# A hybrid decoder block on one core: another form of the norm behind the output projection, and two planner rules

## The chip, the core and the metric

One core of a Trainium2 chip runs the kernel. The metric is the device time of one execution in microseconds. The kernel's engines are called as in the profile: PE (TensorE, matmuls; PEld is its weight load), DVE (VectorE), ACT (ScalarE), POOL (GpSimd) and SP (SyncE, which here only issues DMAs).

## The reference

One layer of a decoder block on x of 512 tokens by 1,024 features, in float32. A vector c gives six modulation vectors; a mixer (a convolution branch and latent attention, gated and merged, then one output projection) and an MLP of width 4,096 follow, each between norms:

```python
mod = silu(c) @ w_ada + b_ada        # shift1, scale1, gate1, shift2, scale2, gate2
h = rms_norm(x, g_pre_mix) * (1.0 + scale1) + shift1
y = token_mixer(h, ...)              # ends in (g_a * y_a + g_b * y_b) @ w_out
x = x + gate1 * rms_norm(y, g_post_mix)

h = rms_norm(x, g_pre_mlp) * (1.0 + scale2) + shift2
y = square(relu(h @ w_mlp_in)) @ w_mlp_out
x = x + gate2 * rms_norm(y, g_post_mlp)
```

`rms_norm(x, g)` is `x * rsqrt(mean(x * x) + eps) * g` over the features.

## The kernel before

**Number format.** Float32 products are made of three matmuls (`mm3`): each operand is split into a high part in fp32r and a low part, and high x high, high x low and low x high are summed in PSUM. The split costs ACT a cast and DVE a subtraction per operand, so nearly all weights and activations pass through ACT and DVE on their way to PE.

**Recording and planning.** No engine is called directly. `act`, `dve`, `pe`, `pool` and `sp` record operations into a `Planner`; `record` (from L262) works out on which earlier operations each one depends, by the regions that it reads and writes, and gives it a cost by a table (`cost`). `plan` (from L340) then simulates the engines: PE takes ready operations by their rank in the program, the others by their due time, worked back from PE's. `issue` sends everything in the order that came out; whatever the operation, its line in the profile is that of the sending call, L421. So a change of a dependency, a cost or a landing time changes the order of instructions on every engine, though not the instructions. Loads are modelled by `o.dma` and a landing time `o.t1`; at most DEPTH of them are in flight on SP.

**Memory.** `fa` hands out pieces of one float32 arena (`f_arena` in the profile), `ra` of an fp32r arena (`r_arena`), `pb` the eight PSUM banks of 512 float32 columns. `stats` and `mod` hold small vectors.

**The stage behind the output projection.** Tokens lie in four row tiles t of 128 (NT = 4), features in KD = 8 blocks k of 128. The product with w_out is made in halves nh of 512 columns: first the halves 0 of all tiles, 96 matmuls of 512 columns; then `late_mod` turns the last modulation vectors (parts 2, 3 and 4 of w_ada) into G1, which is gate1 times the norm's gain, broadcast to 128 rows, and into columns of `mod`; then halves 1, 24 matmuls of 512 columns a tile, 96 in all. When a tile's second half is done, its norm runs, row by row: sum of squares, a power -0.5 on POOL, product with G1, addition to the residual xr, a second norm for the MLP, whose result is transposed on PE (eight 128x128 transposes a tile, four to a PSUM bank, tiles in pairs tp) and evacuated with scale and shift into h2, feature-major, in high and low parts. ACT writes v and the high part, DVE the low part; each covers 256 columns, the pair's tokens.

**The MLP.** The first four blocks of the hidden layer are computed in two steps of 256 tokens, so that they need only the first pair's h2 at first: these are the 256-column matmuls on `r_arena` (360 of them). All later ones have 512 or 256 columns by a Strassen-like scheme. While it runs, `ada_units((5,))` computes the last part of the modulation, gate2, on DVE, from 1 MB loads of two row blocks of w_ada each.

These lines are the norm of tile t before, which the change rewrites (`rstd` is the Identity on ACT with scale and epsilon, and the power on POOL):

```python
                for nh in range(2):
                    act.activation(fa.v(j), pb.v(ys[t, nh]), AF.Square, accum_out=s[:, nh:nh + 1])
```

Of the kernel before, what the change touches and what calls it, by code (L numbers as in the profile page):

```python
# [14 lines left out]
AF = mybir.ActivationFunctionType  # L15
ALU = mybir.AluOpType

P = 128
T = 512
NT = T // P  # L20
D = 1024
KD = D // P
# [33 lines left out]
ADAS = (1, 1, 0, 4)  # L56
KGRP = ((1,), (2,), (3,), (4,), (5,), (6,), (7,))
HL, SQ = 5e3, False
ADD, LATE5 = 2.6, 1
HX, HA, HG, HC = 1.2e5, 1e5, 3e3, 1.1e5  # L60

# [108 lines left out]


class Op:
    __slots__ = ("i", "eng", "fn", "a", "k", "cost", "post", "deps", "succ", "dead", "t0", "t1", "ndep", "ready", "dma", "rank", "hurry", "bufs", "raw")


class Planner:
# [6 lines left out]
    def __init__(self, nc, spaces):  # L183
        self.spaces = spaces
        self.real = dict(pe=nc.tensor, act=nc.scalar, dve=nc.vector, pool=nc.gpsimd, sp=nc.sync)
        self.ops = []
        self.last_w = {}
        self.reads = {}
        self.boost = 0
        self.hurry = 0.0  # L190
        self.after = None
        self.slack = 0.0

    class Engine:
        def __init__(self, plan, name):
# [76 lines left out]
    def record(self, eng, fn, a, k):  # L272
# [3 lines left out]
        outs, ins = [], []  # L276
# [9 lines left out]
        o = Op()  # L286
        o.i, o.eng, o.fn, o.a, o.k = len(self.ops), eng, fn, a, k
        o.succ, o.dma, o.rank, o.hurry = [], None, len(self.ops) - self.boost, self.hurry
        o.cost, o.post = self.cost(eng, fn, outs, ins, k)
        o.post += self.slack if eng == "pool" else 0.0  # L290
        if fn == "dma_start":
            b = 4
# [29 lines left out]
        for nm, units in wr:  # L322
            lw, rs = self.last_w[nm], self.reads[nm]
            for u in units:
                lw[u] = o.i
                rs.pop(u, None)
        deps.discard(o.i)
        if self.after is not None:
            deps.add(self.after)
# [5 lines left out]
    def plan(self):  # L335
# [29 lines left out]
        while len(order) < len(ops):  # L365
# [3 lines left out]
            for e in self.NAMES:  # L369
                if free[e] <= now and heaps[e]:  # L370
                    o = ops[heapq.heappop(heaps[e])[1]]
                    o.t0 = now
                    free[e] = now + o.cost
                    if o.dma:
                        st = max(now + 1100.0, dma_free)
                        dma_free = st + o.dma
                        o.t1 = dma_free + 1100.0
                        landed.append(o.t1)
                        free[e] = max(free[e], landed[-DEPTH])
                    else:  # L380
                        o.t1 = free[e] + o.post
                    order.append(o)
                    for s in o.succ:
                        q = ops[s]
                        q.ndep -= 1
                        q.ready = max(q.ready, o.t1 if (q.eng != o.eng or o.dma) else free[e] if e == "pe" else max(free[e], o.t1 - 30))
                        if not q.ndep:
                            heapq.heappush(future, (q.ready, q.i))
# [37 lines left out]
def tile_hybrid_block(  # L426
# [48 lines left out]
    def emit(past, replay):  # L475
# [713 lines left out]
        def ada_units(parts):  # L1189

            for part in parts:
                acc = ada_acc[part] = fa.alloc(D)
                for u in range(4):
                    b = fa.alloc(2 * D)
                    v = fa.v(b, "p (j n) -> p j n", j=2)
                    sp.dma_start(out=v, in_=w_ada[u * 256:(u + 1) * 256, part * D:(part + 1) * D].rearrange("(j p) n -> p j n", p=P))
                    for jj in range(2):
                        j = u * 2 + jj
                        if j == 0:
# [201 lines left out]
        xr = []  # L1401
# [31 lines left out]
        for tp in range(2):  # L1433
            xn = []
            for t in (2 * tp, 2 * tp + 1):
# [2 lines left out]
                    if t == NT - 1 and k % 2 == 1:  # L1438
                        wo[k // 2].free()
                s = stat(6)  # L1440
                j = fa.alloc(512)
                for nh in range(2):
                    act.activation(fa.v(j), pb.v(ys[t, nh]), AF.Square, accum_out=s[:, nh:nh + 1])
                fa.free(j)
                act.activation(s[:, 2:3], s[:, 0:1], AF.Identity, scale=0.25 / D, bias=epsc[:, 0:1])
                rstd(s[:, 3:4], s[:, 1:2], 0.25 / D, s[:, 2:3])
                y = fa.alloc(D)
                for nh in range(2):
                    sl = slice(nh * 512, (nh + 1) * 512)
                    dve.scalar_tensor_tensor(fa.v(y)[:, sl], pb.v(ys[t, nh]), s[:, 3:4], fa.v(G1)[:, sl], op0=ALU.mult, op1=ALU.mult)  # L1450
                    pb.free(ys[t, nh])
                dve.tensor_tensor(fa.v(xr[t]), fa.v(xr[t]), fa.v(y), ALU.add)
                act.activation(fa.v(y), fa.v(xr[t]), AF.Square, accum_out=s[:, 4:5])
                rstd(s[:, 5:6], s[:, 4:5], 1.0 / D)
                dve.tensor_scalar(fa.v(y), fa.v(xr[t]), s[:, 5:6], None, ALU.mult)
                for nh in range(2):
                    sl = slice(nh * 512, (nh + 1) * 512)
# [12 lines left out]
            for k2 in range(KD // 2):  # L1470
# [5 lines left out]
                for q in range(2):  # L1476
                    k = 2 * k2 + q
                    ps, v = pb.v(b)[:, q * 256:(q + 1) * 256], k4(fa.v(h2f[k // 4]))[:, k % 4, hsl]
                    hb, lb = (ra.v(z)[:, hsl] for z in h2[k])
                    if k == 0:  # L1480
                        act.activation(hb, ps, AF.Identity, scale=mod[:, 3, k:k + 1], bias=mod[:, 2, k:k + 1])
                        dve.tensor_scalar(v, ps, mod[:, 3, k:k + 1], mod[:, 2, k:k + 1], ALU.mult, ALU.add)
                    else:
# [12 lines left out]
        G2, fin = None, []  # L1496

        late = ada_units((5,))

        def blocks_of(wsrc, k0):  # L1500

# [183 lines left out]
        for ch in range(NCH):  # L1685
# [3 lines left out]
            for n0 in range(0, HPC, GRP):  # L1689
# [12 lines left out]
                ws = ws0 if ch == 0 and n0 == 0 else hid_weights(ch * HPC + n0, GRP)  # L1702
                step = 256 if ch == 0 and n0 == 0 else T
                for t0 in range(0, T, step):
                    for i in range(GRP):
                        for k in range(KD):
                            mm3(pb.v(bs[i])[:, t0:t0 + step], ws[i - i % 2, k // 4](k % 4, (i % 2) * P, P), h2s(k, t0, step),
                                k == 0, k == KD - 1)
                for w in ws.values():
# [131 lines left out]
```

## Time and profile before

| | us |
|---|---|
| median of 3 runs | 811.71 (811.28 to 812.33) |
| the profiled execution | 812.9 |
| its span in the profile | 810.8 |
| PE busy | 791.7 (98%) |
| DVE busy | 732.8 (90%) |
| ACT busy | 476.7 (59%) |
| POOL busy | 62.6 (8%) |

The mean granted PE clock was 0.996 of full speed. Some 2.1 us of the execution lie outside the span. In the profile's chain of work that ended last PE has 84% and DVE 9%. In timelines and groups, a row has the operation, output and inputs by name, and the number of instructions; a bracket holds the idle time ahead of it and what ended that. As all operations have line L421 (L433 in the changed kernel, which is twelve lines longer up to there), operations are told apart by engine, names and shapes.

### The profile page before, as it was taken

The numbers are of one execution on the slowest core, as the hardware profiler recorded it, in microseconds if no ns is written. First come the engines' busy times: TensorE is split into PE (matmuls) and PEld (weight loads), VectorE is DVE, ScalarE is ACT, GpSimd is POOL, SyncE is SP. The second block draws the span as 40 slices with busy tenths as digits, with TensorE's granted clock in tenths as the row PEclk, the third lists the DMA queues.
The fourth block names the chain that finished last, engine by engine and source line by source line (L and its number), as shares of the span: only waits on it lengthen the run. The fifth ranks groups of instructions, "written<-read, shape, count | busy, mean of one in ns | idle before, by whom it ended". The sixth has DMA issues, their size and how long they took to land.

```text
span 810.8 us, 11964 instructions
## 1 busy us (share of the span) xinstructions
PE 791.7 (98%) x4450; PEld 689.5 (85%) x4450; DVE 732.8 (90%) x1040; ACT 476.7 (59%) x790; POOL 62.6 (8%) x121
## 2 busy tenths in 40 slices
PE   5999999999999999999999999999999999999996
PEld 2788988889897888888888879988998899889985
DVE  2799999999999999999896578899999968996998
ACT  5555463365885247238243276677667766777842
POOL 2001010000000000000000020001002200320023
PEclk9999999999999999999999999999999999999999
DMA  8999433112252261343798062139826950895095
GB/s 256 314 272 356 142 121 107 53 53 78 92 170 78 79 181 53 104 157 122 291 395 280 1 208 97 60 83 305 314 78 141 272 168 17 179 281 177 1 190 135
DMA packets 100108, 130.99 MB, mean 162 GB/s; under 512 B 8561, under 2 KB 67282, under 8 KB 100050
## 3 DMA queue, kind: packets, MB, share of 16 engines
q1 hardware_dynamic: 93714, 118.69, 44.3%
q0 software_dynamic: 6336, 11.54, 8.8%
q8 instruction: 35, 0.57, 0.3%
q14 instruction: 23, 0.19, 0.1%
HBM read 109.23 MB, written 20.97 MB: 161 GB/s over the span
## 4 chain that ended last, share of the span: by engine, by line
PE 84%; DVE 9%; ACT 2%; issue 2%; DMA 2%; SPq 0%; DVEq 0%; POOLq 0%; POOL 0%
PE psum L421 84%; DVE f_arena L421 5%; DVE r_arena L421 4%; ACT f_arena L421 1%; ACT r_arena L421 1%; DMA rows<-in_g_pre_mix_dram 1%; DMA f_arena<-in_w_in_dram 1%; SPq L421 0%; DVEq L1836 0%; POOLq L1836 0%; DVE mod L421 0%; POOL stats L421 0%; ACT stats L421 0%; DVE stats L421 0%; DVE cols L421 0%
## 5 line engine op out<-in xcount | busy, mean ns | idle before, releaser
L421 PE MATMUL psum<-r_arena 128*128 128x512 f32 (+3 forms) x4108 | 752.3, 344 | 1.8 <-ACT f_arena L421 0.7
L421 PEld LDWEIGHTS psum<-r_arena 128*128 128x128 f32 x4108 | 649.8, 190 | 87.7 <-ACT r_arena L421 1.7
L421 ACT CAST r_arena<-f_arena 128x1024 fp32r<-128x1024 f32 (+4 forms) x249 | 236.2, 967 | 152.8 <-PE psum L421 92.8
L421 DVE TENSOR_TENSOR r_arena<-f_arena,r_arena 128x1024 fp32r<-128x1024 f32 (+5 forms) x259 | 276.1, 1097 | 27.2 <-PE psum L421 15.6
L421 DVE SCALAR_TENSOR_TENSOR f_arena<-f_arena,cw 128x512 f32<-128x512 f32 x240 | 164.9, 745 | 0.0
L421 DVE TENSOR_TENSOR f_arena<-f_arena 128x1024 f32<-128x1024 f32 (+3 forms) x108 | 114.3, 1076 | 3.8 <-ACT f_arena L421 2.4
L421 ACT ACTIVATE f_arena<-f_arena 128x512 f32<-128x512 f32 (+4 forms) x121 | 71.4, 609 | 41.6 <-DVE f_arena L421 40.8
L421 ACT COPY f_arena<-psum 128x512 f32<-128x512 f32 (+4 forms) x107 | 57.5, 550 | 48.3 <-PE psum L421 43.6
L421 DVE SCALAR_TENSOR_TENSOR f_arena<-f_arena,cT 128x256 f32<-128x256 f32 (+1 forms) x70 | 54.3, 800 | 1.5 <-DMA f_arena<-in_w_ada_dram 1.2
L421 POOL DMA_DIRECT2D y_spill<-f_arena x40 | 34.7, 868 | 263.6 <-ACT f_arena L421 263.6
L421 ACT ACTIVATE f_arena<-psum 128x512 f32<-128x512 f32 x43 | 25.3, 594 | 38.8 <-PE psum L421 38.7
L421 PE MATMUL psum<-ident,f_arena 128*128 128x128 f32 (+1 forms) x234 | 33.4, 279 | 5.2 <-DVE f_arena L421 5.2
L421 PEld LDWEIGHTS psum<-ident,f_arena 128*128 128x128 f32 (+1 forms) x234 | 27.4, 143 | 10.9 <-DVE f_arena L421 5.7
L421 DVE TENSOR_TENSOR r_arena<-psum,r_arena 128x512 fp32r<-128x512 f32 (+2 forms) x57 | 35.9, 656 | 0.3
L421 DVE TENSOR_TENSOR f_arena<-psum,f_arena 128x512 f32<-128x512 f32 (+1 forms) x35 | 23.2, 673 | 13.7 <-PE psum L421 13.7
L421 ACT CAST r_arena<-psum 128x512 fp32r<-128x512 f32 (+2 forms) x57 | 29.9, 563 | 8.9 <-PE psum L421 8.6
L421 POOL TENSOR_TENSOR stats<-stats,nhalf 128x1 f32<-128x1 f32 (+1 forms) x17 | 15.9, 942 | 169.6 <-ACT stats L421 159.4
L421 POOL TENSOR_TENSOR lns<-lns,nhalf 128x4 f32<-128x4 f32 x1 | 2.0, 2002 | 249.3 <-DVE lns L421 249.3
L421 ACT ACTIVATE r_arena<-f_arena 128x256 fp32r<-128x256 f32 (+3 forms) x17 | 10.9, 643 | 14.0 <-DVE f_arena L421 11.3
L421 DVE CUSTOM_DVE_ANT_0 f_arena<-psum,mask 128x128 f32<-128x128 f32 (+3 forms) x32 | 14.9, 484 | 0.1
L421 DVE TENSOR_SCALAR f_arena<-f_arena,stats 128x1024 f32<-128x1024 f32 x8 | 6.0, 751 | 8.5 <-POOL stats L421 8.5
L421 DVE SCALAR_TENSOR_TENSOR f_arena<-f_arena 128x512 f32<-128x512 f32 (+1 forms) x18 | 13.1, 748 | 0.2 <-ACT f_arena L421 0.2
(96 smaller groups left out, 204.0 us busy)
## 6 DMA issues: line engine op xcount, KB each, us to landing
f_arena<-in_w_ada_dram SPq DMA_DIRECT2D x16, 1024.0 KB, 6.5
f_arena<-in_w_mlp_in_dram SPq DMA_DIRECT2D x32, 512.0 KB, 6.0
f_arena<-in_w_mlp_out_dram SPq DMA_DIRECT2D x32, 512.0 KB, 5.9
f_arena<-in_w_in_dram SPq DMA_DIRECT2D x24, 512.0 KB, 4.8
y_spill<-f_arena POOLq DMA_DIRECT2D x40, 256.0 KB, 6.4
f_arena<-in_w_ada_dram SPq DMA_DIRECT2D x24, 256.0 KB, 5.9
f_arena<-in_x_dram SPq DMA_DIRECT2D x8, 512.0 KB, 7.1
h_spill<-r_arena SPq DMA_DIRECT2D x16, 256.0 KB, 7.0
```

What stands on the lines that cost most here:

```text
L421: getattr(self.real[o.eng], o.fn)(*o.a, **o.k)
```

## The change

**The norm.** Before, DVE multiplied the PSUM halves by the norm's factor and by G1 in one instruction each, once the power was there, added the result to xr (1,024 wide), ACT squared the sum (1,024 wide), POOL took the second power. Now DVE multiplies both halves by G1 at once (`tensor_tensor`, which needs no statistic) into y; ACT squares PSUM with the scale folded in; after the power two instructions on DVE make y times factor plus xr, half by half; ACT squares half 0 and adds epsilon, and DVE's `tensor_tensor_reduce` squares and sums half 1, starting from ACT's value; POOL takes the power. The scaling by it is as before. The scratch j lies in the fp32r arena.

**The planner.** With EXCL, operations of different engines on one PSUM bank depend on each other in the plan, whatever columns they touch: each waits for the run of operations that another engine had last on the bank. With LAG, the loads by SP into the float32 arena that are recorded after `late = ada_units((5,))`, that is the MLP's, land 3,000 ns later in the plan. **Loads.** With AJ = 1 each 1 MB load of w_ada in `ada_units` becomes two of 512 KB. KOUT and VK have the values that leave the code as it was.

```diff
+EXCL = True
+LAG, AJ = 3000.0, 1
+KOUT, VK = False, (0,)
...
+        o.lag = self.lag if fn == "dma_start" and eng == "sp" and outs[0].tensor.name.startswith("f_arena") else 0.0
...
+        if EXCL:
+            for bank in {u // 2 for nm, units in rd + wr if nm.startswith("psum") for u in units}:
+                runs = self.runs.setdefault(bank, [(None, []), (None, [])])
+                if runs[1][0] != eng:
+                    runs[:] = [runs[1], (eng, [])]
+                deps.update(runs[0][1])
+                runs[1][1].append(o.i)
...
-                        o.t1 = dma_free + 1100.0
+                        o.t1 = dma_free + 1100.0 + o.lag
...
-                    sp.dma_start(out=v, in_=w_ada[u * 256:(u + 1) * 256, part * D:(part + 1) * D].rearrange("(j p) n -> p j n", p=P))
+                    src = w_ada[u * 256:(u + 1) * 256, part * D:(part + 1) * D].rearrange("(j p) n -> p j n", p=P)
+                    for jj in range(0, 2, AJ):
+                        sp.dma_start(out=v[:, jj:jj + AJ], in_=src[:, jj:jj + AJ])
...
-                j = fa.alloc(512)
-                for nh in range(2):
-                    act.activation(fa.v(j), pb.v(ys[t, nh]), AF.Square, accum_out=s[:, nh:nh + 1])
-                fa.free(j)
-                act.activation(s[:, 2:3], s[:, 0:1], AF.Identity, scale=0.25 / D, bias=epsc[:, 0:1])
-                rstd(s[:, 3:4], s[:, 1:2], 0.25 / D, s[:, 2:3])
                 y = fa.alloc(D)
+                j = ra.alloc(512)
                 for nh in range(2):
                     sl = slice(nh * 512, (nh + 1) * 512)
-                    dve.scalar_tensor_tensor(fa.v(y)[:, sl], pb.v(ys[t, nh]), s[:, 3:4], fa.v(G1)[:, sl], op0=ALU.mult, op1=ALU.mult)
+                    act.activation(ra.v(j), pb.v(ys[t, nh]), AF.Square, scale=0.5 * D ** -0.5, accum_out=s[:, nh:nh + 1])
+                    if nh == 0:
+                        act.activation(s[:, 0:1], s[:, 0:1], AF.Identity, bias=epsc[:, 0:1])
+                    dve.tensor_tensor(fa.v(y)[:, sl], pb.v(ys[t, nh]), fa.v(G1)[:, sl], ALU.mult)
                     pb.free(ys[t, nh])
-                dve.tensor_tensor(fa.v(xr[t]), fa.v(xr[t]), fa.v(y), ALU.add)
-                act.activation(fa.v(y), fa.v(xr[t]), AF.Square, accum_out=s[:, 4:5])
-                rstd(s[:, 5:6], s[:, 4:5], 1.0 / D)
+                rstd(s[:, 2:3], s[:, 1:2], 1.0, s[:, 0:1])
+                for nh in range(2):
+                    sl = slice(nh * 512, (nh + 1) * 512)
+                    xs_ = fa.v(xr[t])[:, sl]
+                    dve.scalar_tensor_tensor(xs_, fa.v(y)[:, sl], s[:, 2:3], xs_, op0=ALU.mult, op1=ALU.add)
+                    if nh == 0:
+                        act.activation(ra.v(j), xs_, AF.Square, scale=D ** -0.5, accum_out=s[:, 3:4])
+                        act.activation(s[:, 3:4], s[:, 3:4], AF.Identity, bias=epsc[:, 0:1])
+                    else:
+                        dve.tensor_tensor_reduce(ra.v(j), xs_, xs_, 1.0 / D, s[:, 3:4], ALU.mult, ALU.add, s[:, 4:5])
+                        pool.tensor_tensor(s[:, 5:6], s[:, 4:5], nhalf[:, :1], ALU.pow)
+                ra.free(j)
                 dve.tensor_scalar(fa.v(y), fa.v(xr[t]), s[:, 5:6], None, ALU.mult)
```

What the plan makes of it is seen in the orders. PE behind the output projection, before: the rows of 512 columns are the second halves of the four tiles, 96 in all; the groups of transposes (`ident`) between them are first those of `late_mod` (16), then those of the normalized tiles; the rows of 256 columns are the first MLP matmuls.

```order
166 L421 MATMUL psum<-ident,f_arena 128x128 x16
167 L421 MATMUL psum<-r_arena 128x512 x62
168 L421 MATMUL psum<-ident,f_arena 128x128 x4
169 L421 MATMUL psum<-r_arena 128x512 x2
170 L421 MATMUL psum<-ident,f_arena 128x128 x2
171 L421 MATMUL psum<-r_arena 128x512
172 L421 MATMUL psum<-ident,f_arena 128x128 x2
173 L421 MATMUL psum<-r_arena 128x512 x21
174 L421 MATMUL psum<-ident,f_arena 128x128 x8
175 L421 MATMUL psum<-r_arena 128x512 x10
176 L421 MATMUL psum<-r_arena 128x256 x30
177 L421 MATMUL psum<-ident,f_arena 128x128 x8
```

PE at the same place in the changed kernel:

```order
160 L433 MATMUL psum<-ident,f_arena 128x128 x16
161 L433 MATMUL psum<-r_arena 128x512 x53
162 L433 MATMUL psum<-ident,f_arena 128x128 x8
163 L433 MATMUL psum<-r_arena 128x512 x20
164 L433 MATMUL psum<-ident,f_arena 128x128 x8
165 L433 MATMUL psum<-r_arena 128x512 x23
166 L433 MATMUL psum<-r_arena 128x256 x16
167 L433 MATMUL psum<-ident,f_arena 128x128 x8
168 L433 MATMUL psum<-r_arena 128x256 x50
169 L433 MATMUL psum<-ident,f_arena 128x128 x8
```

Tile 0's transposes stood behind 62 of the 96 matmuls, in three pieces, tile 1's behind 85; now behind 53 and 73, each in one piece. Tiles 2 and 3 follow behind 16 and 66 short matmuls; it was 30 and 68 before.

DVE at the norms of tiles 0 and 1, before (`stats` holds the row statistics):

```order
444 L421 SCALAR_TENSOR_TENSOR f_arena<-psum,stats,f_arena 128x512 x2
445 L421 TENSOR_TENSOR f_arena<-f_arena 128x1024
446 L421 TENSOR_SCALAR f_arena<-f_arena,stats 128x1024
447 L421 SCALAR_TENSOR_TENSOR f_arena<-psum,stats,f_arena 128x512 x2
448 L421 TENSOR_TENSOR f_arena<-f_arena 128x1024
449 L421 TENSOR_TENSOR r_arena<-f_arena,r_arena 128x1024
450 L421 TENSOR_SCALAR f_arena<-f_arena,stats 128x1024
```

DVE there in the changed kernel (ISA with `stats` is the reduction, and the row behind it the read of its sum):

```order
470 L433 TENSOR_TENSOR f_arena<-psum,f_arena 128x512
471 L433 SCALAR_TENSOR_TENSOR f_arena<-f_arena,stats 128x512 x2
472 L433 ISA r_arena,stats<-f_arena,stats 128x512
473 L433 ISA stats 128x1
474 L433 TENSOR_SCALAR f_arena<-f_arena,stats 128x1024
475 L433 TENSOR_TENSOR f_arena<-psum,f_arena 128x512
476 L433 SCALAR_TENSOR_TENSOR f_arena<-f_arena,stats 128x512 x2
477 L433 ISA r_arena,stats<-f_arena,stats 128x512
478 L433 ISA stats 128x1
479 L433 TENSOR_SCALAR f_arena<-f_arena,stats 128x1024
```

The addition of 1,024 columns is gone; a product from PSUM and a reduction have come. Only one product a tile stands here: those of the halves 0 have moved up among `late_mod`'s operations.

PE in its first part, before (`cT` is c in columns; these matmuls make the first modulation vectors):

```order
6 L421 MATMUL psum<-ident,f_arena 128x128 x6
7 L421 MATMUL psum<-ones,f_arena 128x1 x2
8 L421 MATMUL psum<-f_arena,cT 1x256 x8
9 L421 MATMUL psum<-ident,f_arena 128x128 x6
10 L421 MATMUL psum<-ones,f_arena 128x1 x2
```

And now:

```order
6 L433 MATMUL psum<-ident,f_arena 128x128 x6
7 L433 MATMUL psum<-ones,f_arena 128x1 x2
8 L433 MATMUL psum<-ident,f_arena 128x128 x5
9 L433 MATMUL psum<-f_arena,cT 1x256 x8
10 L433 MATMUL psum<-ident,f_arena 128x128 x12
```

Five transposes have moved ahead of the matmuls with `cT`.

More of the change, by code (lines that the diff above doesn't have):

```diff
@@ L172 @@
 class Op:
-    __slots__ = ("i", "eng", "fn", "a", "k", "cost", "post", "deps", "succ", "dead", "t0", "t1", "ndep", "ready", "dma", "rank", "hurry", "bufs", "raw")
+    __slots__ = ("i", "eng", "fn", "a", "k", "cost", "post", "deps", "succ", "dead", "t0", "t1", "ndep", "ready", "dma", "lag", "rank", "hurry", "bufs", "raw")
 class Planner:
@@ L191, in __init__ @@
         self.after = None
-        self.slack = 0.0
+        self.runs = {}
+        self.lag = self.slack = 0.0
     class Engine:
@@ L1479, in emit @@
                     hb, lb = (ra.v(z)[:, hsl] for z in h2[k])
-                    if k == 0:
+                    if k in VK:
                         act.activation(hb, ps, AF.Identity, scale=mod[:, 3, k:k + 1], bias=mod[:, 2, k:k + 1])
@@ L1498, in emit @@
         late = ada_units((5,))
+        plan.lag = LAG
         def blocks_of(wsrc, k0):
@@ L1704, in emit @@
                 for t0 in range(0, T, step):
-                    for i in range(GRP):
-                        for k in range(KD):
+                    for i, k in ([(i, k) for k in range(KD) for i in range(GRP)] if step < T and KOUT
+                                 else [(i, k) for i in range(GRP) for k in range(KD)]):
+                        if True:
                             mm3(pb.v(bs[i])[:, t0:t0 + step], ws[i - i % 2, k // 4](k % 4, (i % 2) * P, P), h2s(k, t0, step),
```

## The prediction

> **What bounds the kernel now.** I read the page first, for the busy shares, then PE's waits, then PE's row in stretches, and last the chain inside one stretch. The page:
>
> ```profile
> span 810.8 us, 11964 instructions
> PE 791.7 (98%) x4450; PEld 689.5 (85%) x4450; DVE 732.8 (90%) x1040; ACT 476.7 (59%) x790; POOL 62.6 (8%) x121
> ```
>
> PE is busy for 791.7 of 810.8 us. So the change can only gain what PE loses: in waits, in a slower clock, in a tail. PE's waits in the whole span (total us, times, longest), the larger ones:
>
> ```profile
> PE psum L421 <- DVE f_arena L421: 5.2, 1, 5.2
> PE psum L421 <- DMA c<-in_c_dram: 2.3, 1, 2.3
> PE psum L421 <- ACT f_arena L421: 1.1, 2, 0.7
> PE psum L421 <- DMA rows<-in_g_pre_mix_dram: 1.0, 1, 1.0
> PE psum L421 <- DVE r_arena L421: 0.6, 1, 0.6
> PE psum L421 <- DVE mod L421: 0.4, 1, 0.4
> PE psum L421 <- ACT r_arena L421: 0.4, 1, 0.4
> ```
>
> The 5.2, the 2.3, the 1.0 and the 0.4 for mod stand in the first 25 us, while inputs land. Of the rest, 0.7 for ACT f_arena and 0.6 for DVE r_arena stand at one place, behind the norm. The stretches around it (PE busy, PEld, DVE, ACT, POOL, granted clock, DMA share, GB/s):
>
> ```profile
> 420.00:440.00 20.00, 20.00 (x90) 16.58 (x89) 19.81 (x23) 9.89 (x12) 0.00 (x0) 1.00 1.06 368
> 460.00:475.70 15.70, 15.70 (x74) 12.98 (x74) 9.53 (x13) 6.88 (x17) 3.70 (x5) 1.00 0.27 100
> 475.70:479.50 3.80, 3.78 (x20) 2.63 (x18) 3.80 (x6) 3.80 (x8) 0.42 (x1) 1.00 0.68 235
> 479.50:483.00 3.50, 2.03 (x12) 1.41 (x11) 3.13 (x6) 3.44 (x11) 1.40 (x1) 1.00 0.69 235
> 483.00:486.40 3.40, 3.40 (x16) 3.40 (x17) 3.34 (x5) 3.40 (x8) 0.53 (x2) 0.51 0.85 272
> 486.40:493.00 6.60, 6.60 (x58) 6.60 (x57) 5.37 (x8) 2.09 (x5) 1.88 (x1) 0.99 0.57 192
> 580.00:600.00 20.00, 20.00 (x169) 20.00 (x168) 18.18 (x18) 14.06 (x20) 0.00 (x0) 1.00 0.45 160
> ```
>
> A 512-column matmul takes 20/90 = 0.222 us, a 256-column one 20/169 = 0.118. In 479.5 to 483 PE did 12 short matmuls, worth 1.42 of 3.50 us: 2.08 lost. In 483 to 486.4 it did 16, worth 1.89 of 3.40, at clock 0.51: 1.51 lost. Together **3.59 us**, the loss of this stage. The waits are the cause; the slow clock follows them. PE there:
>
> ```profile
> 476.14 1.09 PE L421 MATMUL psum<-ident,f_arena 128*128 128x128 f32 x8
> 480.54 1.71 PE L421 MATMUL psum<-r_arena 128*128 128x256 f32 x9 [0.60 <-DVE r_arena L421]
> 482.97 4.15 PE L421 MATMUL psum<-r_arena 128*128 128x256 f32 x20 [0.72 <-ACT f_arena L421]
> ```
>
> The transposes of row tile 1 start at 476.14; behind them stand, by the order of before, ten long matmuls (2.2 us), and then MLP matmuls that need h2, evacuated from these transposes by ACT and DVE. So h2 is late, because the normalized tile 1 was.
>
> **The norm, tile by tile.** The chain before, in DVE's rows and ACT's (the last two are ACT's evacuation of h2, quoted for later):
>
> ```profile
> 462.84 1.41 DVE L421 SCALAR_TENSOR_TENSOR f_arena<-psum,stats,f_arena 128x512 f32<-128x512 f32 x2 [0.92 <-POOL stats L421]
> 464.28 1.23 DVE L421 TENSOR_TENSOR f_arena<-f_arena 128x1024 f32<-128x1024 f32 x1
> 468.14 0.75 DVE L421 TENSOR_SCALAR f_arena<-f_arena,stats 128x1024 f32<-128x1024 f32 x1 [2.63 <-POOL stats L421]
> 475.33 0.75 DVE L421 TENSOR_SCALAR f_arena<-f_arena,stats 128x1024 f32<-128x1024 f32 x1 [0.44 <-POOL stats L421]
> ...
> 461.16 0.60 ACT L421 ACTIVATE f_arena<-psum 128x512 f32<-128x512 f32 x1 [6.95 <-PE psum L421]
> 461.66 0.19 ACT L421 ACTIVATION_READ_ACCUMULATOR f_arena<-psum 128x1 f32 x1
> 461.88 0.29 ACT L421 ACTIVATE stats<-stats 128x1 f32<-128x1 f32 x1
> 465.54 1.06 ACT L421 ACTIVATE f_arena<-f_arena 128x1024 f32<-128x1024 f32 x1 [3.37 <-DVE f_arena L421]
> 466.60 0.60 ACT L421 ACTIVATE f_arena<-psum 128x512 f32<-128x512 f32 x1
> 481.92 1.00 ACT L421 ACTIVATE f_arena<-psum,mod 128x256 f32<-128x256 f32 x2
> 482.82 0.71 ACT L421 CAST r_arena<-f_arena 128x256 fp32r<-128x256 f32 x2
> ```
>
> From the last Square on PSUM to the normalized tile: tile 0 461.16 to 468.89, 7.7 us; tile 1 466.60 to 476.08, 9.5 us. Nothing runs beside it: Square, power, two products, a 1.23 us addition, a 1.06 us Square, power, scaling.
>
> Prices of the new instructions, from the nearest forms in the run (count, total us, mean ns, idle before):
>
> ```profile
> L421 DVE TENSOR_TENSOR f_arena<-psum,f_arena 128x512 f32<-128x512 f32 x33 | 22.3, 689 | 13.7 <-PE psum L421 13.7
> L421 DVE SCALAR_TENSOR_TENSOR f_arena<-f_arena,stats 128x512 f32<-128x512 f32 x8 | 5.7, 755 | 0.1
> L421 DVE CUSTOM_DVE_ANT_0 r_arena<-f_arena,stats 128x512 fp32r<-128x512 f32 x3 | 2.2, 758 | 0.0
> L421 DVE DVE_READ_ACCUMULATOR2_ANT stats<- 128x1 f32 x4 | 0.4, 92 | 0.0
> L421 DVE SCALAR_TENSOR_TENSOR f_arena<-psum,stats,f_arena 128x512 f32<-128x512 f32 x8 | 5.6, 746 | 1.4 <-POOL stats L421 1.4
> L421 DVE TENSOR_SCALAR f_arena<-psum,mod 128x256 f32<-128x256 f32 x2 | 1.1, 545 | 1.7 <-ACT f_arena L421 1.7
> ```
>
> Counted from the Square's start: the first power is there at 1.7, as before (462.84 - 461.16; the Identity now comes earlier, which I leave out). The product with G1 is 0.69 long and is meanwhile done, at 0.7 beside the Square or at 0.60 + 0.69 = 1.3 behind it. The second is likelier: the last row above is DVE reading one half of a bank and waiting for ACT, whose read of the other half ended then. Both are under 1.7, so it costs nothing. Two multiply-adds end at 1.7 + 2 x 0.755 = 3.2. ACT squares half 0 from 2.45: a 512-wide Square, its read and Identity are 0.60 + 0.19 + 0.29, to 3.5. DVE's reduction of half 1 waits 0.3 for that seed and ends, with its read, at 3.5 + 0.76 + 0.09 = 4.4. From a statistic's end to DVE through POOL took 462.84 - 462.17 = 0.67; the scaling starts at 5.05 and ends at **5.8**. So tile 0 is 1.9 us earlier and tile 1, were nothing in its way, 3.7; tile 1's last matmul comes 24 x 0.222 = 5.3 us after tile 0's, while DVE holds tile 0 until 5.8, so 0.5 go, and I take 0.3 more for queueing: about **2.9**. Seen against the 1.32 us of waits listed (or 2.08 lost), this suffices, if PE's order uses it.
>
> It does: the transposes of tiles 0 and 1 now stand behind 53 and 73 of the 96 long matmuls (62 and 85 before). Tile 0's last matmul is the 24th, so 29 x 0.222 = 6.4 us pass against a chain of 5.8; tile 1's is the 48th, 25 x 0.222 + 1.1 for tile 0's eight transposes = 6.6 against 5.8. And 23 long matmuls, not 10, now cover the evacuation: 13 x 0.222 = 2.9 us more. Evacuating two k blocks took ACT 1.00 + 0.71 us, so eight blocks need some 6.9 us from the transposes; 23 x 0.222 + 21 x 0.118 = 7.6 us pass until the last block is first read. Tight, since tile 2's Square (0.6 + 0.19) also stands in ACT's way. I leave **0.5 us** of waits, between 0 and the old 1.3. The slow stretch I take as gone with them.
>
> How sure are the 1.51 us? They come from one execution, at 812.9 us, which is 1.2 above the median of the timed ones. The Trainium skill ("TensorE: Matmul & The Clock Gate", Part 1) states that the gate judges a free-running window of about 3.4 us, so that the same kernel is slowed for differing stretches from run to run. By that sentence the stretch could be missing in the median run, and the sum would be 1.5 smaller. The trace agrees with it in part only: the stretch at 0.51 is 3.4 us long, but it followed waits of 1.3 us, not an idle window. I count the 1.51 in full; the other case is the first rival.
>
> DVE's work: per tile 2 x 0.689 + 2 x 0.755 + 0.758 + 0.092 for 2 x 0.746 + 1.22, +1.0 us, 4.1 in all. Of it the products of the first halves, 4 x 0.689 = 2.8, stand earlier, where DVE idles. In 460 to 493 DVE was busy for 9.53 + 3.80 + 3.13 + 3.34 + 5.37 = 25.2 of 33 us; now 26.5 of 29.3 (33 less the gain). It fits, with less room than before: the cover that could fail.
>
> **The other edits.** Six groups of transposes become four in this stage. A change of kind costs about 0.09 us: a long matmul between two groups took 0.31, not 0.222:
>
> ```profile
> 470.62 0.48 PE L421 MATMUL psum<-r_arena 128*128 128x512 f32 x1
> 470.93 0.38 PE L421 MATMUL psum<-ident,f_arena 128*128 128x128 f32 x2
> ...
> 465.54 0.83 SPq L421 DMA_DIRECT2D out_dram<-f_arena  x2
> ...
> DVE r_arena L421 <- PE psum L421: 6.8, 6, 1.7
> ```
>
> That is **-0.2**. At the start five transposes now stand ahead of the matmuls that waited 0.4 for mod: 5 x 0.14 (1.09/8) = 0.7 us covers it, **-0.4**, between 0 and -0.4. Halved w_ada loads are 16 more issues on SP at 0.83/2 = 0.42 us, 6.7 us spread over hundreds: nothing; without cover one late load, 0.4. The bank rule and the landing margin issue no instruction; they alter order alone. PE's remaining small waits (0.4 for ACT r_arena, 0.4 more for ACT f_arena) may go or grow: 0, between -1 and +1. In the MLP PE doesn't wait (20.00 of 20.00 us in the row of 580 to 600), so a margin can gain nothing there. Could it lose? DVE's orders differ by at most five places, and DVE itself waits for PE to free buffers (last row above, of 640 to 720: 6.8 us), so it works ahead: 0, at worst +1.2, one 1024-wide operation. The tail holds the same operations: 0.
>
> Sum: -3.6 + 0.5 - 0.2 - 0.4 = **-3.7 us**. The profiled run took 812.9, 2.1 more than its span; it should come to 809.2, the span to 807.1. The median was 811.7, so **808.0**. A measurement here can tell about 0.2%, 1.6 us.
>
> **The rivals.** *The clock's share isn't gained (0.17).* Whether a stall halves the clock may hang on where it falls, so that the timed runs of before mostly lack the slow stretch; or what is left of the waits still trips it. The 1.51 us drop out of the sum: 3.7 - 1.5 = 2.2, 809.5. For it: the profiled execution is slower than the timed ones by nearly that much. Against: the stall that comes before it stands in the order of every run alike. *The stall moves (0.11).* Tiles 2 and 3 are now transposed behind 16 and 66 short matmuls, where 30 and 68 stood; 14 x 0.118 = 1.7 us less for tile 2's chain. If tile 2 comes late by all of that and the clock follows (1.5), 3.2 of 3.6 is given back: 811.3. *More goes (0.12).* All of PE's small waits vanish, the two of 0.4 too, and nothing is left in the stage: 808.0 - 0.5 - 0.8 = 806.7. For it: the whole order is planned anew. Against: the same could open others.
>
> *DVE becomes the bound; slower (0.08).* DVE's queue is in order. In each of tiles 2 and 3 it now stands at the first power (1.0), the seed (0.3) and the second power (0.7): 2 us, while the low parts of h2 queue behind. If both are in PE's path, PE loses 4 us and, with a slow stretch after each, 3 more: 7.0 for 3.6, less the 0.6: 811.7 + 2.8 = 814.5. It decides once these waits exceed 3.6 + 0.6 - 3.0 = 1.2 us. For it: 26.5 of 29.3 us busy. Against: the planner puts low parts and weight parts between; the old chain had the same two waits for powers, of 0.92 and 2.63.
>
> **How the numbers follow.** Forecast 0.52, the rivals as given. The forecast's own range is 806.5 to 809.8: 0 to 1.3 us of waits, mid waits by 1 each way. Down to 805.5 takes in the third rival and 1.2 more, up to 811.0 the first with its waits; beyond lie the stall that moves and the slower case, 0.2. Faster by over 1.6 us: the forecast, the third, and most of the first, 0.78; within: 0.14; slower: 0.08.
>
> **What would show it.** Right: the clock at 1.00 through the stage; PE's waits behind the norm at 0.5 or less; 5.8 us from Square to scaling; PE's first 512-column matmul 0.4 earlier; no wait in the MLP. Wrong: a stretch near 0.5 at the transposes of tile 2, DVE waiting for POOL or ACT statistics while PE waits for DVE r_arena, or any PE wait past 490.

## The result and the profile after

| | before | changed |
|---|---|---|
| median, us | 812.25 (811.28 to 814.07, 6 runs) | 808.14 (807.52 to 809.09, 6 runs) |
| the profiled execution, us | 812.9 | 807.76 |
| its span, us | 810.8 | 805.6 |

The ratio of the times is 0.9948, 95% interval 0.9935 to 0.9962: 4.1 us less, by the medians. (The kernel before has six runs here; the prediction had seen three of them, with 811.71.)

The page of the changed kernel, its first rows:

```profile
span 805.6 us, 12015 instructions
PE 789.3 (98%) x4450; PEld 687.6 (85%) x4450; DVE 735.8 (91%) x1052; ACT 476.6 (59%) x790; POOL 59.6 (7%) x121
```

PE's waits in the whole span:

```profile
PE psum L433 <- DVE f_arena L433: 5.6, 2, 5.2
PE psum L433 <- DMA c<-in_c_dram: 2.4, 1, 2.4
PE psum L433 <- DVE r_arena L433: 0.2, 1, 0.2
```

Three kinds of wait are left of nine, and the two waits behind the norm (0.7 and 0.6) are gone; the 0.2 stands before 250 us. The two stretches that lost 3.59 us before:

```profile
479.50:483.00 3.50, 3.47 (x30) 3.27 (x30) 3.50 (x8) 3.50 (x9) 0.54 (x1) 1.00 0.19 49
483.00:486.40 3.40, 3.40 (x29) 3.33 (x29) 3.40 (x6) 2.37 (x4) 0.66 (x1) 1.00 0.98 355
```

PE does 30 matmuls (eight of them transposes) and 29 there instead of 12 and 16, at clock 1.00. What PE does around them, with no idle time in brackets anywhere:

```profile
466.23 1.03 PE L433 MATMUL psum<-ident,f_arena 128*128 128x128 f32 x8
467.02 4.80 PE L433 MATMUL psum<-r_arena 128*128 128x512 f32 x20
471.65 1.03 PE L433 MATMUL psum<-ident,f_arena 128*128 128x128 f32 x8
472.44 7.38 PE L433 MATMUL psum<-r_arena 128*128 128x512 f32 x39
479.85 1.09 PE L433 MATMUL psum<-ident,f_arena 128*128 128x128 f32 x8
```

And the chain of tile 0, ACT's rows and then DVE's:

```profile
459.85 0.60 ACT L433 ACTIVATE r_arena<-psum 128x512 fp32r<-128x512 f32 x1 [6.09 <-PE psum L433]
462.31 0.64 ACT L433 ACTIVATE r_arena<-f_arena 128x512 fp32r<-128x512 f32 x1 [1.44 <-DVE f_arena L433]
...
460.57 0.69 DVE L433 TENSOR_TENSOR f_arena<-psum,f_arena 128x512 f32<-128x512 f32 x1 [1.00 <-ACT r_arena L433]
461.52 1.41 DVE L433 SCALAR_TENSOR_TENSOR f_arena<-f_arena,stats 128x512 f32<-128x512 f32 x2 [0.27 <-POOL stats L433]
463.39 0.75 DVE L433 CUSTOM_DVE_ANT_0 r_arena<-f_arena,stats 128x512 fp32r<-128x512 f32 x1 [0.46 <-ACT stats L433]
464.82 0.75 DVE L433 TENSOR_SCALAR f_arena<-f_arena,stats 128x1024 f32<-128x1024 f32 x1 [0.67 <-POOL stats L433]
470.25 0.75 DVE L433 TENSOR_SCALAR f_arena<-f_arena,stats 128x1024 f32<-128x1024 f32 x1 [0.66 <-POOL stats L433]
```

From the Square to the end of the scaling: 459.85 to 465.57, 5.7 us, where it was 7.7. The first bracket of DVE holds the wait on the shared bank: up to 459.85 both engines wait for PE, and for the last 0.72 of the 1.00 us the product stands until ACT's Square has read the same columns. The page "PSUM — Partial Sum Buffer" of the Trainium skill (section "PSUM bank collisions raise a hardware error") says that two engines on one bank and quadrant must be kept apart, reads included; this trace agrees, as the two reads don't overlap. The program keeps them apart whether the plan counts on it or not: without the rule on banks the same product has a wait of 0.94.

**Where the time went.** For every profile below I add up what PE loses: for each matmul the time from its start to the next one's start, less the median of that time for matmuls of its form, in us by stretch of the span. It holds waits, slow clock and changes of kind alike; the first two waits of the program, 2.3 and 5.2 us before, stand outside it, as the first matmul has nothing ahead of it and is alone of its form.

| run | 0 to 30 | 30 to 440 | 440 to 500 | 500 to 803 | sum |
|---|---|---|---|---|---|
| before | 5.5 | 4.0 | 4.4 | 0.1 | 14.0 |
| changed | 3.9 | 4.3 | 0.5 | 0.0 | 8.6 |

The difference of the two profiles is 5.4 us: 3.9 behind the norm, 1.6 at the start. The timed medians differ by 4.1; what of the two parts is in them is taken up behind the experiments.

### The profile page after: what moved, and what is told of

It reads as the page before. It is cut to its first block, busy times and chain, and to the rows that moved or that the text cites. A ratio compares the mean times of both kernels' runs of the same rounds, so it can differ in the third digit from the quotient of the medians.

```text
span 805.6 us, 12015 instructions
## 1 busy us (share of the span) xinstructions
PE 789.3 (98%) x4450; PEld 687.6 (85%) x4450; DVE 735.8 (91%) x1052; ACT 476.6 (59%) x790; POOL 59.6 (7%) x121
## 4 chain that ended last, share of the span: by engine, by line
PE 84%; DVE 11%; issue 2%; ACT 2%; DMA 1%; POOL 0%; SPq 0%; DVEq 0%; ACTq 0%
PE psum L433 84%; DVE f_arena L433 6%; DVE r_arena L433 5%; ACT r_arena L433 1%; DMA rows<-in_b_ada_dram 1%; ACT f_arena L433 1%; DMA r_arena<-h_spill 0%; SPq L433 0%; POOL lns L433 0%; DVEq L1859 0%; POOL stats L433 0%; DVE lns L433 0%; DVE stats L433 0%; DVEq L433 0%; ACTq L433 0%
## 5 line engine op out<-in xcount | busy, mean ns | idle before, releaser
L433 DVE TENSOR_TENSOR f_arena<-f_arena 128x1024 f32<-128x1024 f32 (+3 forms) x104 | 110.1, 1072 | 3.7 <-DMA f_arena<-in_w_mlp_in_dram 3.2
L433 ACT ACTIVATE f_arena<-f_arena 128x512 f32<-128x512 f32 (+3 forms) x117 | 67.0, 593 | 17.2 <-DVE f_arena L433 16.2
L433 DVE TENSOR_TENSOR f_arena<-psum,f_arena 128x512 f32<-128x512 f32 (+1 forms) x43 | 28.7, 677 | 12.1 <-PE psum L433 9.3
L433 PE MATMUL psum<-ident,f_arena 128*128 128x128 f32 x234 | 33.0, 280 | 5.2 <-DVE f_arena L433 5.2
L433 ACT ACTIVATE f_arena<-psum 128x512 f32<-128x512 f32 x35 | 20.5, 596 | 28.4 <-PE psum L433 21.2
L433 PEld LDWEIGHTS psum<-ident,f_arena 128*128 128x128 f32 x234 | 27.3, 143 | 11.0 <-DVE f_arena L433 5.5
L433 POOL TENSOR_TENSOR stats<-stats,nhalf 128x1 f32<-128x1 f32 (+1 forms) x17 | 12.3, 722 | 169.5 <-ACT stats L433 147.5
L433 ACT ACTIVATE r_arena<-f_arena 128x512 fp32r<-128x512 f32 (+3 forms) x21 | 13.5, 645 | 16.1 <-DVE f_arena L433 13.8
L433 ACT ACTIVATE r_arena<-psum 128x512 fp32r<-128x512 f32 x12 | 7.2, 598 | 24.5 <-PE psum L433 24.5
```

The source lines that it names most:

```text
L433: getattr(self.real[o.eng], o.fn)(*o.a, **o.k)
```

## The experiments

The question was whether the shorter norm brings these 3.9 us by itself, or the planner's rules do. A short edit and the four stretches stand with each run; ratios are to the kernel before, on the same chip.

**The norm alone.**

```diff
-EXCL = True
-LAG, AJ = 3000.0, 1
+EXCL = False
+LAG, AJ = 0.0, 2
```

> The new norm with none of the planner's rules and with 1 MB loads of w_ada (EXCL off, LAG 0, AJ 2); the computation is the same. Its PE order has the transposes of tiles 0 and 1 behind 53 and 73 of the 96 long matmuls, as the changed kernel has, and the start as the kernel before. Theory (the shorter norm, by way of the order that it allows, brings nearly all): no PE wait in the stage, clock 1.00 there, about 3.6 to 4 us under before, ratio 0.9950 to 0.9957. Rival 1 (the planner's rules bring it): within 1 us of before, ratio 0.999 or more, with PE waits of 1 us or more behind the norm. Rival 2 (half is the new order at the start): 2 us, ratio 0.9975.

Measured: 812.75 us, ratio 1.0017 (1.0000 to 1.0033). Lost: 3.5, 5.3, 2.0, 4.0. So the norm alone gains nothing. Behind the norm the loss falls from 4.4 to 2.0, though not to nothing; and the MLP, free of waits in the profile before, now loses 4.0. PE's rows with idle time (the first two from around the transposes, the others from the MLP):

```profile
482.05 1.09 PE L433 MATMUL psum<-ident,f_arena 128*128 128x128 f32 x8 [0.47 <-DVE f_arena L433]
485.70 4.54 PE L433 MATMUL psum<-r_arena 128*128 128x256 f32 x35 [0.36 <-DVE r_arena L433]
...
583.67 151.58 PE L433 MATMUL psum<-r_arena 128*128 128x256 f32 x960 [1.68 <-DVE f_arena L433]
736.85 29.05 PE L433 MATMUL psum<-r_arena 128*128 128x256 f32 x240 [1.60 <-ACT f_arena L433]
```

My theory fails here: less is lost behind the norm, but as much is given back in a place that the norm doesn't touch, by a plan that came out otherwise. The numbers of rival 1 come out (within 1 us of before by the medians, and three waits of 1.0 us together behind the norm, the third of 0.21 at 495.8), but it doesn't name the MLP, and the next run takes up whether the rules bring the gain by themselves.

**The old norm with the planner's rules.** The norm's lines of before stand in the changed kernel (three of the changed lines are shown).

```diff
-                    dve.tensor_tensor(fa.v(y)[:, sl], pb.v(ys[t, nh]), fa.v(G1)[:, sl], ALU.mult)
...
+                    dve.scalar_tensor_tensor(fa.v(y)[:, sl], pb.v(ys[t, nh]), s[:, 3:4], fa.v(G1)[:, sl], op0=ALU.mult, op1=ALU.mult)
+                dve.tensor_tensor(fa.v(xr[t]), fa.v(xr[t]), fa.v(y), ALU.add)
```

> The changed kernel with the old norm; the planner's rules and the halved loads stay. The plan now puts tile 0's transposes behind 71 and tile 1's behind 93 of the 96 long matmuls, with 3 long matmuls behind the last. Theory: the stage loses again what it lost before, 3.6 us, and up to 1.5 more, since 3 long matmuls cover less than 10 while the transposes come 8 matmuls later; the start's gain of about 0.4 stays; so 0 to 1.5 us over before, ratio 1.000 to 1.002, with waits behind the norm and a stretch of slow clock. Rival 1 (the planner's rules bring it): as the changed kernel, ratio 0.995.

Measured: 812.65 us, ratio 1.0006 (0.9996 to 1.0017). Lost: 6.2, 4.0, 5.3, 0.2. As expected: the stage loses what it lost before and 0.9 more, so the rules alone don't bring the gain. PE behind the last transposes, and three stretches with the granted clock third from the end:

```profile
481.19 0.74 PE L433 MATMUL psum<-r_arena 128*128 128x256 f32 x3 [1.25 <-ACT f_arena L433]
482.70 0.39 PE L433 MATMUL psum<-r_arena 128*128 128x256 f32 x1 [0.77 <-ACT r_arena L433]
483.75 4.93 PE L433 MATMUL psum<-r_arena 128*128 128x256 f32 x25 [0.67 <-DVE f_arena L433]
...
481.36:484.77 3.41, 1.98 (x11) 1.39 (x12) 2.98 (x6) 3.41 (x10) 2.06 (x2) 1.00 0.73 244
484.77:488.18 3.41, 3.41 (x19) 3.41 (x18) 3.41 (x8) 3.41 (x10) 0.60 (x1) 0.50 0.60 221
488.18:491.59 3.41, 3.41 (x31) 3.41 (x31) 2.98 (x4) 0.57 (x1) 1.86 (x1) 1.00 0.00 1
```

The slow clock came again with the waits, for 3.41 us, as long as before. In this kernel it is the rule: 9 of its 12 runs have a mean granted clock of 0.995 or less. How often the kernel before has it is taken up below.

**Without the rule on banks.**

```diff
-EXCL = True
+EXCL = False
```

> The changed kernel without the rule on PSUM banks. The stage's order is nearly the same (53 and 73), the start is that of the kernel before (no transposes ahead of the second group of matmuls with cT). Theory: all of the stage's gain stays, 0.4 us of wait for mod comes back: ratio 0.9950 to 0.9957, 0 to 0.4 us over the changed kernel. Rival (real waits of ACT and DVE on one bank, which the plan doesn't see without the rule, cost PE): waits behind the norm of 0.5 us or more and 1 to 2 us over the changed kernel, ratio 0.997.

Measured: 812.06 us, ratio 1.0000 (0.9991 to 1.0009). Lost: 3.6, 7.0, 2.0, 0.0. Neither expectation holds in full: the rival named the waits behind the norm, and the whole gain goes, in the profiles 1.5 us behind the norm and 2.7 before 440 us. The rows behind the norm are short waits for the low parts of h2:

```profile
483.05 0.85 PE L433 MATMUL psum<-r_arena 128*128 128x256 f32 x5 [0.19 <-DVE r_arena L433]
487.03 4.53 PE L433 MATMUL psum<-r_arena 128*128 128x256 f32 x35 [0.24 <-DVE r_arena L433]
497.08 1.10 PE L433 MATMUL psum<-r_arena 128*128 128x256 f32 x7 [0.34 <-DVE r_arena L433]
```

**Without margin and halved loads.**

```diff
-LAG, AJ = 3000.0, 1
+LAG, AJ = 0.0, 2
```

> The changed kernel with no landing margin and 1 MB loads of w_ada. Tile 0's transposes stand behind 59 matmuls, tile 1's behind 73. Theory: neither edit is on PE's path; the time is that of the changed kernel within 0.5 us, ratio 0.9943 to 0.9953, and PE has no wait in the MLP. Rival (the margin keeps a late load out of PE's path): PE waits for a DMA or for a split weight in the MLP, 1 us or more, ratio 0.996 or more.

Measured: 810.81 us (807.88 to 813.14), ratio 0.9979 (0.9966 to 0.9993). Lost: 3.5, 4.1, 0.6, 4.4. The rival holds. PE's longest two waits in the MLP, and DVE's wait for a load, from 640 to 800 us:

```profile
653.43 78.86 PE L433 MATMUL psum<-r_arena 128*128 128x256 f32 x504 [0.92 <-ACT f_arena L433]
733.69 29.05 PE L433 MATMUL psum<-r_arena 128*128 128x256 f32 x240 [1.40 <-ACT f_arena L433]
...
DVE f_arena L433 <- DMA f_arena<-in_w_mlp_in_dram: 6.9, 2, 3.5
```

DVE stands at a weight that hasn't landed, for 3.5 us at the longest, and what the plan has put behind it on DVE comes later. In the changed kernel DVE's only wait for such a load, from 560 to 800 us, is 0.6. Three more kernels take this apart.

**Without the margin alone, twice.**

```diff
-LAG, AJ = 3000.0, 1
+LAG, AJ = 0.0, 1
```

> The changed kernel with the landing margin at 0; the loads of w_ada stay halved. PE's whole order is the changed kernel's, DVE's and ACT's differ in the MLP. Two runs have shown that without margin and halved loads PE loses 4 us in the MLP behind ACT's and DVE's splitting of weights that landed late. Theory (the margin is what keeps this out): no wait in the stage behind the norm, 3 to 4.5 us lost between 500 and 800, ratio to the kernel before 0.998 to 1.000. Rival (the halved loads keep it out, by landing earlier): no wait in the MLP, ratio 0.9943 to 0.9953.

Measured: 813.03 us (808.58 to 814.76, 12 runs), ratio 0.9998 (0.9984 to 1.0012). The profiled execution was the fastest of the twelve; it lost 3.1, 4.4, 0.5, 1.6. A second profile of the same kernel:

> The changed kernel without the landing margin, profiled once more: its profiled execution was 808.6 us, the lowest of twelve, whose median was 813.0, so that its profile lacks most of the loss. Theory (weights land late by a varying amount, and without margin PE waits for their splitting in the MLP): an execution of 811 us or more shows 2 us or more lost between 500 and 800, and none beyond 0.5 behind the norm. Rival (the loss of the timed runs lies elsewhere): the MLP loses under 1.5 us again, and an execution of 811 us or more has its loss before 500.

Measured: 810.23 us, lost 3.7, 4.6, 0.5, 2.4. Its waits behind 500 us:

```profile
631.88 78.92 PE L433 MATMUL psum<-r_arena 128*128 128x512 f32 x504 [0.61 <-DVE r_arena L433]
711.42 49.90 PE L433 MATMUL psum<-r_arena 128*128 128x512 f32 x377 [0.61 <-DVE r_arena L433]
```

This execution stayed under the 811 us for which theory and rival were given, so neither is settled in full; the MLP's 2.4 is more than the rival allows. Both executions lose only in the MLP what they lose more than the changed kernel after 30 us, within 0.4 us, and the slower one loses more there. That the margin is needed is shown by the times, with one edit between 813.03 and 808.14. An execution of 813 us, the median, wasn't profiled, and in these two DVE waits little for loads (1.4 and 2.2 us from 500 to 800), so what makes PE late in the slow ones is open in part.

**Without the halved loads alone.**

```diff
-LAG, AJ = 3000.0, 1
+LAG, AJ = 3000.0, 2
```

> The changed kernel with 1 MB loads of w_ada; the margin stays at 3,000 ns. Theory (the margin does it): no wait over 0.3 us in the MLP, none in the stage behind the norm either, ratio 0.9943 to 0.9955. Rival (the halved loads do it): 3 us or more lost between 500 and 800, ratio 0.998 or more.

Measured: 807.80 us (806.92 to 809.16, 6 runs), ratio 0.9939 (0.9923 to 0.9955). Lost: 4.4, 4.2, 0.5, 1.0. As the theory has it, but for 0.9 us just behind 500. The halved loads bring no gain that can be measured, nor do they without the margin (813.03 with them, 810.81 without); the margin does it.

**The margin alone, on the kernel before.** The old norm, EXCL off, 1 MB loads, and

```diff
+LAG, AJ = 3000.0, 2
```

> The kernel before with the landing margin alone (old norm, no rule on banks, 1 MB loads). Theory (the margin gains only where a plan without it would lose in the MLP, and the kernel before loses nothing there): the MLP stays free of waits, the stage behind the norm keeps its loss (its order has the transposes of tiles 0 and 1 behind 73 and 85 of the 96 long matmuls), 3 to 5 us; ratio 0.999 to 1.001. Rival (the margin is a gain by itself): ratio 0.997 or less.

Measured: 811.29 us, ratio 0.9990 (0.9977 to 1.0003). Lost: 6.0, 5.1, 2.0, 0.3. The ratio is as expected, the stage lost less than the 3 to 5 us that I gave: with 11 long matmuls behind the last transposes the waits were two short ones, and the clock stayed up:

```profile
483.62 0.50 PE L433 MATMUL psum<-r_arena 128*128 128x256 f32 x2 [0.20 <-ACT r_arena L433]
484.77 1.34 PE L433 MATMUL psum<-r_arena 128*128 128x256 f32 x9 [0.66 <-ACT f_arena L433]
```

The margin is no gain by itself. But here the old norm loses 2.0 behind the norm, no more than the new norm alone: so the fall from 4.4 to 2.0 in the first experiment may be the other plan's as well as the shorter chain's.

**The same order with a longer chain.** Three powers more on POOL per tile, x to the power 1, issued behind the second power and unknown to the plan, so that every engine's order stays.

```diff
             getattr(self.real[o.eng], o.fn)(*o.a, **o.k)
+            for _ in range(0 if o.again is None else EXTRA):
+                self.real["pool"].tensor_tensor(o.a[0], o.a[0], o.again, ALU.pow)
```

> The changed kernel with its order kept to the instruction, but with three powers more on POOL behind the second power of each tile (x to the power 1, unknown to the plan). Two powers in a row took 1.38 us before, so each chain is 2.1 us longer; tile 0's and tile 1's transposes have some 0.65 us of slack. Theory (this order pays only because the chain is as short as it is): PE waits 1.4 us at tile 0's transposes, up to 1.8 at tile 1's, which DVE serves later, and some behind them; 3 to 4 us of waits and, behind waits of more than 1.3 us, a stretch of half clock that costs 1.5; in all 3 to 6 us over the changed kernel, ratio to the kernel before 0.9985 to 1.0025. Rival (the chain has slack, only PE's order counts): under 1 us over the changed kernel, ratio 0.996 or less.

Measured: 814.42 us, ratio 1.0018 (1.0007 to 1.0029). Lost: 5.8, 4.1, 5.4, 0.9. As the theory says, 4.9 us more behind the norm than in the changed kernel, at all four tiles:

```profile
469.32 1.09 PE L435 MATMUL psum<-ident,f_arena 128*128 128x128 f32 x8 [1.10 <-DVE f_arena L435]
475.72 1.09 PE L435 MATMUL psum<-ident,f_arena 128*128 128x128 f32 x8 [0.74 <-DVE f_arena L435]
484.99 1.09 PE L435 MATMUL psum<-ident,f_arena 128*128 128x128 f32 x8 [1.03 <-DVE f_arena L435]
493.63 1.09 PE L435 MATMUL psum<-ident,f_arena 128*128 128x128 f32 x8 [1.52 <-DVE f_arena L435]
...
490.00:494.00 4.00, 2.48 (x21) 2.28 (x20) 2.33 (x4) 0.00 (x0) 2.54 (x4) 1.00 0.93 325
```

The chain's length is what this order lives on. The half clock that I expected behind waits of over 1.3 us didn't come: the last row, around the wait of 1.52, has 1.00, and so have the 4 us behind it.

**A wider margin.**

```diff
-LAG, AJ = 3000.0, 1
+LAG, AJ = 6000.0, 1
```

> The changed kernel with a margin of 6,000 ns. The first two transpose groups stand as in the changed kernel, tile 2's come behind 9 short matmuls, not 16. Theory (3,000 ns already clears the MLP; more only makes loads be planned earlier and everything else more crowded): no wait in the MLP, ratio 0.994 to 0.997, no better than the changed kernel; tile 2's earlier transposes may wait some tenths. Rival (late landings still cost in timed runs of the changed kernel): ratio under 0.994, 1 us under the changed kernel.

Measured: 808.96 us, ratio 0.9956 (0.9943 to 0.9970). Lost: 3.9, 3.9, 0.8, 0.2. As expected, tile 2's transposes wait a little, and nothing is gained:

```profile
479.15 1.09 PE L433 MATMUL psum<-ident,f_arena 128*128 128x128 f32 x8 [0.36 <-DVE f_arena L433]
```

**The rule on banks from the last stage on.**

```diff
-        if EXCL:
+        if self.excl:
...
+        plan.excl = EXCL
         G1 = late_mod()
```

> The changed kernel with the rule on banks only from the stage behind the output projection on. Without the rule at all PE lost 1.2 us more at 30 to 100 us, 1.4 more at 350 to 440 and 1.5 more behind the norm. Theory (the rule pays at each place by planning for waits that ACT and DVE have on a shared bank in any case): the first two losses stay, the third goes: some 2.5 us over the changed kernel and 1.5 under the one without the rule, ratio 0.9970 to 0.9985. Rival (what differs between the plans is chance, not the rule): loss behind the norm of 1.5 us or more though the rule holds there, or under 1 us before 440 though it doesn't.

Measured: 808.41 us, ratio 0.9954 (0.9938 to 0.9970). Lost: 4.1, 3.6, 0.4, 0.3. Half of my theory falls, and the rival's second condition is met. Behind the norm the loss goes with the rule, as expected. But before 440 us, where the rule doesn't hold in this kernel, only 3.6 us are lost, less than with it (4.3), and not the 7.0 of the kernel without any rule. So those 2.7 us weren't the rule's: they belong to one plan, and another plan under the same rules there doesn't have them. How the one plan came by them isn't settled.

## Why the prediction came out right, point by point

**The sum.** Forecast -3.7 us, measured -4.1 by the medians, inside the range. The terms:

- *The stage behind the norm, -3.6 + 0.5 - 0.2 = -3.3.* In the profiles right, a little small: -3.9. The 3.59 of the two rows was itself small: of their 12 and 16 matmuls one is the end of a long one and one stands in both rows. From the first short one's start at 479.56 to 486.49 there are 26, and 6.93 - 26 x 0.118 = 3.9. The 0.5 us of waits left over, taken because the evacuation's cover seemed tight (6.9 us of ACT and the Square in 7.6), weren't there: PE has no wait from 440 to 500.
- *The chain.* Forecast 5.8 us from Square to scaling, measured 5.7 for tile 0, and for tile 1 from 465.29 to 471.00 the same. The product behind the Square was to end at 1.3 us and ended at 461.26 - 459.85 = 1.4; the wait for the seed was to be 0.3 and was 0.46; from statistic to DVE through POOL 0.67, as taken. The longer chain with the same order shows that these numbers decide.
- *The start, -0.4.* Not to be told. In the orders with the transposes ahead, the wait of 0.4 us for mod is gone. But the start loses anything from 3.1 to 6.2 us in the thirteen profiles; the lowest, 3.1, and the highest, 6.2, have the same order there. Eight profiles with the new order average 4.3, five with the old 4.5, so that the 1.6 us between the first two are chance in the main.
- *The slow clock, 1.51 counted in full.* Right for the profiled execution: the clock stays at 1.00 in the changed kernel. For the timed runs it was wrong in the main. Each run's mean granted clock is on record. In all thirteen profiles the clock also falls to half for the last 2.4 to 5.9 us of the span, behind PE's last matmul; the eleven that have no other slow stretch have a mean of 0.996 to 0.998. One stretch of 3.41 us at half clock takes 3.41 x 0.5 / 810 = 0.002 more, and the two profiles with one have 0.996. Of 75 later runs of the kernel before, 50 have 0.997 or 0.998, too much for such a stretch by this reckoning, and average 812.0 us; 11 have 0.995 or less, and average 813.7; 14 have 0.996 and can't be told. The changed kernel's six have 0.997 or 0.998. So by the clock most runs of before, and with them the median one, lack the slow stretch, which is the condition of the first rival.
- *DVE's room.* It sufficed: DVE is busy for 735.8 us, 3.0 more than before, and PE waits for nothing behind the norm.

**Where luck comes in.** The first rival's condition holds, and its time, 809.5, doesn't. Without the slow stretch some 2.4 us of the 3.9 are left for the median run, and 4.1 were measured: most of the rest must stand somewhere in runs of the kernel before that weren't profiled. Its start, or an MLP that loses more than the 0.1 of the one profile, as the kernels without margin do, are possible; neither is shown. So the hit of 0.4 us is in part luck: 1.5 us were counted that most runs don't have, and something of about that size was missed. Of the other terms, the 0.5 of waits wasn't there and the 0.4 at the start can't be told; as they had opposite signs, the sum hardly shows it.

**The step that failed, without harm to the sum.** "The bank rule and the landing margin issue no instruction; they alter order alone", and "a margin can gain nothing there". Against the kernel before nothing contradicts this: the margin alone measured 0.9990 (0.9977 to 1.0003). But it isn't true of the change. Without the margin the new plan takes 813.0 us (810.8 with 1 MB loads); the profiles show 1.6 to 4.4 us of that in the MLP, where PE waits for weights that ACT and DVE split too late. Without the rule on banks it takes 812.1, and with the norm alone 812.8 against 810.8 for norm and rule without the margin. Behind the norm both kernels without the rule lose 2.0, and every kernel with new norm and rule whose chain was not lengthened 0.8 or less. But the 2.7 us that the changed kernel without the rule loses before 440 us aren't the rule's, as the last experiment shows. I worked out the new order's cover with the order in hand, and the rules were already in it. I credited the norm with what norm and rules bring together: the kernels that lack the norm, the margin or the whole rule measured 0.9979 to 1.0017.

**The rivals.** *The clock's share isn't gained* had its condition right and its time wrong, as said above. *The stall moves* was right about where a stall could come back: tile 2's transposes wait 0.36 us with the wider margin and 0.47 with the norm alone. The larger loss of the norm alone, in the MLP, it doesn't name. *More goes* came near: nothing is left in the stage, though small waits before 440 us remain. *DVE becomes the bound* didn't happen. But its mechanism, operations that queue on DVE behind one that waits, is seen in the MLP of the kernels without margin and with 1 MB loads, where DVE waits up to 3.5 us for a weight.

**A better version?** None was found. The changed kernel without the halved loads measured 0.9939 (0.9923 to 0.9955), against 0.9948 (0.9935 to 0.9962): the intervals overlap, and the halved loads can be left out at no cost.

## What to carry to other kernels

Where a list schedule sets the order, an edit's worth can't be read from the edit's own stage alone: with the norm alone, 2.4 us less were lost where it was made, and the new plan gave 3.9 back in a stage that the edit doesn't touch. Price an order with all of the rules that made it, test each rule by leaving it out, and compare where PE loses time stage by stage before believing a change of the total. Before a loss that one profile shows goes into a forecast of timed runs, look whether the timed runs have it: here their mean clock told. A stage that runs free of waits without a safety margin may owe that to one plan's chance; the next plan shows whether the margin is needed.

## What the runs showed of the hardware

The clock doesn't go by the longest wait. In the thirteen profiles it fell twice in mid-run, both times to 0.50 for 3.41 us. The windows of 3.41 us ahead of and at the slow stretch, before (the old norm's stand above), and a window with a longer wait in the kernel with the longer chain, which is followed by full clock:

```profile
479.66:483.07 3.41, 1.97 (x11) 1.37 (x11) 2.97 (x7) 3.41 (x10) 1.47 (x2) 1.00 0.68 229
483.07:486.48 3.41, 3.41 (x16) 3.41 (x17) 3.41 (x5) 3.41 (x8) 0.46 (x1) 0.50 0.83 265
...
490.80:494.21 3.41, 1.89 (x16) 1.69 (x16) 1.74 (x3) 0.11 (x1) 1.82 (x3) 1.00 0.86 291
494.21:497.62 3.41, 3.41 (x31) 3.41 (x30) 3.41 (x7) 3.41 (x10) 0.00 (x0) 1.00 0.71 202
```

Waits of 0.60 and 0.72 us (before), and of 1.25, 0.77 and 0.67 us (old norm), were followed by half clock; a single wait of 1.52 us was not. PE's busy time doesn't part them either: 1.97 and 1.98 us against 1.89. The number of matmuls that begin in the window would (10 and 10 against 14), but three windows are too few for a rule. "TensorE: Matmul & The Clock Gate" (Part 1) of the Trainium skill names an idle window of about 3.4 us as the condition; the length agrees with the 3.41 us of the slow stretches, but here the clock fell behind windows in which PE was busy for more than half of the time.

The first 30 us vary by up to 3 us between profiles in which PE has the same order there (3.1 to 6.2 us lost), most of the 4.1 us that the whole change brings.
